# A fused low-rank update on one core: the first two stores wait for TensorE's third group instead of for their sums alone

## The chip, the core and the metric

The kernel runs on one core of a Trainium2 chip. Its time is the device time of one execution in microseconds (us); several executions are taken and their median counts. A profile of one further execution gives the trace. In it PE is TensorE (matmul), PEld its weight load, DVE is VectorE, ACT is ScalarE, POOL is GpSimd and SP is SyncE, which here computes nothing: it issues every transfer between the memory (HBM) and the on-chip buffer (SBUF). The transfers themselves are carried out by the core's 16 DMA engines.

## The reference

```python
batch, seq, d_model, r = 16, 512, 768, 16
# x: float32 [16, 512, 768], A: [768, 16], B: [16, 768], scale = 0.5

def reference(x, A, B, scale):
    lora = np.matmul(np.matmul(x, A), B)
    return (x + scale * lora).astype(np.float32)
```

The input x has 8192 rows of 768 float32 numbers, 25.2 MB. All of it is read once, and a result of the same size is written once. A and B are small.

## The kernel before

**Tiles and groups.** The 8192 rows are cut into 64 tiles of 128 rows, and eight tiles make a group, so there are eight groups (0 to 7). A tile takes 3 KB in each of the 128 partitions. SBUF holds 48 tiles of x at a time (`ROOM`); the last 16 tiles reuse the room of the first 16. Results are formed in place, in the room of their x.

**Transfers.** `LOADS` lists eight loads of 2, 6, 8, 8, 8, 16, 8 and 8 tiles (loads 0 to 7), `STORES` five stores of 8, 8, 16, 16 and 16 tiles (stores 0 to 4). A tile is 384 KB, so 8 tiles are 3072 KB and 16 tiles 6144 KB. Each transfer is one instruction of SP, issued in this order: loads 0 and 1, three pieces of A, B, loads 2 to 5, store 0, store 1, then load 6 (after store 0 has landed, s_out0), load 7 (after store 1 has landed, s_out1), then stores 2, 3 and 4. Loads 6 and 7 wait because they overwrite the tiles that stores 0 and 1 read. Store 0 holds group 0, store 1 group 1, store 2 groups 2 and 3, store 3 groups 4 and 5, store 4 groups 6 and 7. Load 5 brings groups 4 and 5, load 6 group 6, load 7 group 7.

**One group.** ACT and POOL narrow half a group each to float16 (L182, each waits for the group's load). DVE turns the eight tiles in blocks (L238). TensorE projects them with A in 24 matmuls (L269) and signals s_y. ACT spreads and scales the small result (L226, s_spread). TensorE then raises it with B, pair by pair: a group has four pairs of tiles (`PAIRS` is 4), four matmuls for each pair into one of two PSUM buffers (L290), and after each pair it raises the semaphore s_lora by one. DVE adds each pair to x in place (L243, `summed`). s_lora counts up over the whole kernel: 4 after group 0, 8 after group 1, 10 when pairs 0 and 1 of group 2 have been raised. TensorE takes the raising of group g in two halves, with half of the projection of group g + 1 behind each.

**Semaphores around the change.** `s_sum` is raised by DVE when the last pair of a store's groups has been added. `s_free[p]` tells TensorE that pair p has been added, so that its PSUM buffer may be overwritten. For the last pair of a group that ends a store, DVE raises s_sum instead, and SP passes it on: it waits for s_sum and then increments `s_free[PAIRS - 1]` (L145 and the lines around it). TensorE waits for that increment before it raises the second pair of the next group. So SP stands between DVE and TensorE at the end of groups 0, 1, 3 and 5, and both the wait and the increment are part of `store` in this kernel, ahead of the transfer's instruction (L146).

**SP's engine is in order.** What stands behind a wait on SP is not issued until the wait ends. The transfers it has issued run by themselves.

Of the kernel before, what the change touches and what calls it, by code (L numbers as in the profile page):

```python
# [28 lines left out]
def kernel(  # L29
# [20 lines left out]
    PAIRS = GROUP // 2  # L50
# [32 lines left out]
    def sem(name):  # L83
        sems.append(nc.alloc_semaphore(name))
        return sems[-1]
# [10 lines left out]
    def memory(t2, i, s, n):  # L96
        S = PARTS[i]
        return t2[ds(parts[i], S * P), :].rearrange("(p s) d -> p s d", s=S)[:, ds(s, n), :]

    def held(i, s, n):  # L100
        return tiles(where.index((i, s)), n)

    def tiles(t, n):
        return x_all[:, ds(t % ROOM, n), :]
# [15 lines left out]
    s_y, s_spread, s_lora = sem("s_y"), sem("s_spread"), sem("s_lora")  # L120
# [7 lines left out]
    STORES = [(0, 0, 8), (1, 0, 8), (2, 0, 16), (3, 0, 16), (4, 0, 16)]  # L128
# [6 lines left out]
    def on_sync(e):  # L135
        def load(k):
            ld = LOADS[k]
            e.dma_start(out=held(*ld), in_=memory(x2, *ld)).then_inc(s_load[k], 16)  # L138

        def store(k, done):  # L140
            st = STORES[k]
            e.wait_ge(s_sum, k + 1)
            if STORED[k] + 1 < NG:

                e.sem_inc(s_free[PAIRS - 1], 1)  # L145
            e.dma_start(out=memory(out2, *st), in_=held(*st)).then_inc(done, 16)  # L146

        load(0)
        load(1)
        e.wait_ge(s_ready, 1)  # L150
        blocks = A.rearrange("(c e) r -> c (e r)", e=64)
        for c in range(SETS):
            e.dma_start(
                out=a_rows[c : SET * SET : SET, :], in_=blocks[ds(c * SET, SET), :]
            ).then_inc(s_a, 16)
        e.wait_ge(s_brows, 1)
        e.dma_start(out=b_rows[0 : R * APART : APART, :], in_=B).then_inc(s_b, 16)
        for k in range(2, len(LOADS) - 2):
            load(k)

        for p in range(2, PAIRS):
            e.sem_inc(s_free[p], 1)
        store(0, s_out0)
        store(1, s_out1)
        e.wait_ge(s_out0, 16)
        load(len(LOADS) - 2)
        e.wait_ge(s_out1, 16)
        load(len(LOADS) - 1)
        for k in range(2, len(STORES)):
            store(k, s_out)  # L170

    here = set()
# [88 lines left out]
    def on_tensor(e):  # L261
# [57 lines left out]
        for p in range(PAIRS):  # L319
            raised(p)  # L320

    on_sync(nc.sync)
    on_gpsimd(nc.gpsimd)
    on_scalar(nc.scalar)
# [46 lines left out]
```

## Time and profile before

| what | value |
|---|---|
| time, median of 3 runs | 124.05 us (123.84 to 124.35) |
| the profiled execution's own time | 124.01 us |
| its span, first to last instruction | 122.2 us |
| busy: DVE | 81.7 us (67%) |
| busy: PE | 52.3 us (43%) |
| busy: ACT | 37.4 us (31%) |
| busy: POOL | 28.4 us (23%) |
| moved by the one DMA queue | 50.43 MB, 413 GB/s over the span |
| group 0's sums end on DVE | 32.7 us |
| group 1's sums end on DVE | 42.6 us |
| group 2's raising begins on PE | 43.2 us |
| last sums end on DVE | 101.2 us |

The span is the time between the first and the last recorded instruction; the 1.8 us beside it lie before and after. Busy shares are means over the whole span and say little by themselves: an engine can be busy 67% of the time and still set the pace for half of it. A transfer has three times that matter: its issue on SP, the moment its packets begin to move, and its landing, when its semaphore is complete. The list of DMA issues gives the first and the last; what lies between is read from the order in which transfers land and from the records of packets.

### The profile page before, as it was taken

The numbers are of one execution on the slowest core, as the hardware profiler recorded it, in microseconds if no ns is written. First come the engines' busy times: TensorE is split into PE (matmuls) and PEld (weight loads), VectorE is DVE, ScalarE is ACT, GpSimd is POOL, SyncE is SP. The second block draws the span as 40 slices with busy tenths as digits, with TensorE's granted clock in tenths as the row PEclk, the third lists the DMA queues.
The fourth block names the chain that finished last, engine by engine and source line by source line (L and its number), as shares of the span: only waits on it lengthen the run. The fifth ranks groups of instructions, "written<-read, shape, count | busy, mean of one in ns | idle before, by whom it ended". The sixth has DMA issues, their size and how long they took to land.

```text
span 122.2 us, 885 instructions
## 1 busy us (share of the span) xinstructions
PE 52.3 (43%) x322; PEld 30.4 (25%) x322; DVE 81.7 (67%) x42; ACT 37.4 (31%) x43; POOL 28.4 (23%) x24
## 2 busy tenths in 40 slices
PE   0000239487457547746745735974674340000000
PEld 0000026253233424424423322642442110000000
DVE  0002850599999999999999979999995991000000
ACT  4002938526408311835340093553004000000000
POOL 7631638026008001705300080440000000000000
PEclk9999999999999999999999996799999955555555
DMA  3999999999998996999999999999899899899890
GB/s 60 420 434 428 451 426 410 459 418 418 483 515 354 418 515 257 467 410 434 442 410 451 426 418 491 426 499 418 370 499 418 370 499 434 354 515 434 386 467 0
DMA packets 1928, 50.43 MB, mean 413 GB/s; under 512 B 236, under 2 KB 236, under 8 KB 392
## 3 DMA queue, kind: packets, MB, share of 16 engines
q1 hardware_dynamic: 1928, 50.43, 96.7%
HBM read 25.26 MB, written 25.17 MB: 413 GB/s over the span
## 4 chain that ended last, share of the span: by engine, by line
DMA 39%; DVE 28%; PE 7%; ACT 3%; issue 3%; POOL 2%; SPq 0%; DVEq 0%
DMA x_sb<-in_x_dram 20%; DMA out_dram<-x_sb 19%; DVE x_sb L243 18%; DVE xt L238 10%; PE ps_yt L269 5%; ACT xn L182 3%; POOL xn L182 2%; PE lora_ps L290 1%; SPq L138 0%; SPq L366 0%; DVEq L256 0%; SPq L145 0%; SPq L133 0%
## 5 line engine op out<-in xcount | busy, mean ns | idle before, releaser
L243 DVE TENSOR_TENSOR x_sb<-x_sb,lora_ps 128x1536 f32<-128x1536 f32 x32 | 53.7, 1733 | 1.4 <-PE lora_ps L290 1.4
L290 PE MATMUL lora_ps<-b_mm,y_bd 128*128 128x512 f16 (+1 forms) x128 | 26.5, 343 | 22.7 <-issue 15.0
L182 ACT CAST xn<-x_sb 128x3072 f16<-128x3072 f32 (+1 forms) x9 | 23.4, 2609 | 36.8 <-DMA x_sb<-in_x_dram 24.2
L238 DVE STREAM_TRANSPOSE xt<-xn 128x3072 f32<-128x3072 f32 (+1 forms) x9 | 27.0, 3004 | 6.7 <-PE ps_yt L269 5.5
L269 PE MATMUL ps_yt<-xt,w_bd 128*128 128x256 f16 x192 | 26.5, 291 | 11.5 <-DVE xt L238 11.5
L182 POOL CAST xn<-x_sb 128x3072 f16<-128x3072 f32 (+1 forms) x8 | 20.7, 2586 | 45.9 <-DMA x_sb<-in_x_dram 23.3
L269 PEld LDWEIGHTS ps_yt<-xt,w_bd 128*128 128x128 f16 x192 | 19.2, 102 | 19.5 <-issue 14.6
L290 PEld LDWEIGHTS lora_ps<-b_mm,y_bd 128*128 128x128 f16 x128 | 11.1, 100 | 36.0 <-issue 18.1
L226 ACT ACTIVATE y_bd<-ps_yt 32x256 f16<-32x256 f32 x32 | 12.0, 374 | 18.3 <-PE ps_yt L269 18.0
L231 DVE STREAM_TRANSPOSE a_t<-a_rows 32x1024 f32<-32x1024 f32 x1 | 1.9, 1945 | 11.4 <-DMA a_rows<-in_A_dram 11.4
L302 PE MATMUL lora_ps<-b_half,pick 128*128 128x512 f16 (+1 forms) x2 | 0.8, 504 | 12.6 <-POOL b_half L200 12.6
L302 PEld LDWEIGHTS lora_ps<-b_half,pick 128*128 128x128 f16 x2 | 0.1, 102 | 12.6 <-issue 12.6
L208 POOL COPY w_bd<-w_one 32x384 f16<-32x384 f16 x4 | 2.0, 500 | 0.2
L200 POOL CAST b_half<-b_rows 128x768 f16<-128x768 f32 x1 | 0.8, 827 | 4.4 <-DMA b_rows<-in_B_dram 4.4
L182 ACT ACT_TABLE_LOAD x1 | 1.3, 1283 | 0.9 <-SPq L133 0.9
L190 POOL MEMSET w_bd<- 128x1536 f32 x1 | 1.4, 1372 | 0.0
L202 POOL CAST w_one<-a_t 32x384 f16<-32x384 f32 x1 | 0.9, 852 | 0.9 <-DVE a_t L231 0.9
L187 POOL MEMSET a_rows<- 32x1024 f32 x1 | 0.9, 941 | 0.5 <-SPq L133 0.5
L219 ACT CAST b_mm<-lora_ps 128x768 f16<-128x768 f32 x1 | 0.8, 798 | 0.0
L188 POOL MEMSET b_rows<- 128x768 f32 x1 | 0.7, 727 | 0.0
L191 POOL MEMSET y_bd<- 128x512 f32 x1 | 0.5, 514 | 0.0
L193 POOL TENSOR_SCALAR_AFFINE_SELECT pick<-pick 128x128 f16<-128x128 f16 x1 | 0.3, 298 | 0.0
(5 smaller groups left out, 0.6 us busy)
## 6 DMA issues: line engine op xcount, KB each, us to landing
out_dram<-x_sb SPq DMA_DIRECT2D x3, 6144.0 KB, 23.6
x_sb<-in_x_dram SPq DMA_DIRECT2D x5, 3072.0 KB, 14.6
x_sb<-in_x_dram SPq DMA_DIRECT2D x1, 6144.0 KB, 42.2
out_dram<-x_sb SPq DMA_DIRECT2D x2, 3072.0 KB, 21.5
x_sb<-in_x_dram SPq DMA_DIRECT2D x1, 2304.0 KB, 9.9
x_sb<-in_x_dram SPq DMA_DIRECT2D x1, 768.0 KB, 4.7
a_rows<-in_A_dram SPq DMA_DIRECT2D x3, 16.0 KB
b_rows<-in_B_dram SPq DMA_DIRECT2D x1, 48.0 KB, 7.5
```

The costliest lines, as they stand in the source:

```text
L182: ins = copy(out=xn[:, ds(first, n), :], in_=tiles(t, n))
L187: e.memset(a_rows[0:Q], 0.0).then_inc(s_ready, 1)
L190: e.memset(w_bd.rearrange("p c k m -> p (c k m)").bitcast(fp32), 0.0)
L202: e.tensor_copy(out=w_one.rearrange("i (c e) k r -> i c e (k r)", c=SETS), in_=a_t[0:Q].rearrange("i k r (e c) -> i c e (k r)", c=SET)[:, ...
L208: e.tensor_copy(out=w_bd[ds(b * Q, Q), :, :, ds(b * Q, R)], in_=w_one).then_inc(s_w, 1)
L226: last = e.mul(out=y_bd[q, :, q], in_=y_ps[q, :, :], mul=sc)
L231: e.transpose(out=a_t[0:Q].rearrange("i k r c -> i (k r) c"), in_=a_rows[0:Q].rearrange("c (i k r) -> c (k r) i", k=2, r=R),).then_inc(s_r ...
L238: return e.transpose(out=ts[0], in_=ts[1])
L243: ins = e.tensor_tensor(out=xs, in0=xs, in1=lora[p % 2], op=mybir.AluOpType.add)
L269: mm = e.matmul(y_ps, w_bd[:, c, k, :], xv[:, :, c, :, k], start=(m == 0), stop=(m == MMS - 1),)
L290: mms.append(e.matmul(t[:, k, ds(n0, w)], y_bd[:, 2 * p + k, :], b_mm[:, ds(n0, w)], start=True, stop=True,))
L302: last = e.matmul(lora[0][:, 0, ds(n0, w)], pick.rearrange("p b r -> p (b r)"), b_half[:, ds(n0, w)], start=True, stop=True,)
```

## The change

The wait for a store's sums, and the increment that SP passes on to TensorE, become a function of their own, `summed`. For stores 0 and 1 both calls of `summed` now come first, then a wait until s_lora has reached 2 x 4 + 2 = 10, and only then are both stores issued. For stores 2 to 4 each `summed` stands directly ahead of its store, as it did. Transfers, sizes, buffers and the other engines' programs are the same.

```diff
+        def summed(k):
+            e.wait_ge(s_sum, k + 1)
+            if STORED[k] + 1 < NG:
+
+                e.sem_inc(s_free[PAIRS - 1], 1)
+
         def store(k, done):
             st = STORES[k]
-            e.wait_ge(s_sum, k + 1)
-            if STORED[k] + 1 < NG:
-
-                e.sem_inc(s_free[PAIRS - 1], 1)
             e.dma_start(out=memory(out2, *st), in_=held(*st)).then_inc(done, 16)
...
         for p in range(2, PAIRS):
             e.sem_inc(s_free[p], 1)
+        summed(0)
+        summed(1)
+
+
+        e.wait_ge(s_lora, 2 * PAIRS + 2)
         store(0, s_out0)
         store(1, s_out1)
         e.wait_ge(s_out0, 16)
...
         load(len(LOADS) - 1)
         for k in range(2, len(STORES)):
+            summed(k)
             store(k, s_out)
```

More of the change, by code (lines that the diff above doesn't have):

```diff
@@ L138, in load @@
             e.dma_start(out=held(*ld), in_=memory(x2, *ld)).then_inc(s_load[k], 16)
-        def store(k, done):
-            st = STORES[k]
+        def summed(k):
             e.wait_ge(s_sum, k + 1)
@@ L145, in store @@
                 e.sem_inc(s_free[PAIRS - 1], 1)
+        def store(k, done):
+            st = STORES[k]
             e.dma_start(out=memory(out2, *st), in_=held(*st)).then_inc(done, 16)
```

## The prediction

> **What bounds the kernel now.** I read the page first: the DMA row of its slices, the queue totals and the shares of the chain of waits.
>
> ```profile
> DMA  3999999999998996999999999999899899899890
> ...
> q1 hardware_dynamic: 1928, 50.43, 96.7%
> HBM read 25.26 MB, written 25.17 MB: 413 GB/s over the span
> ...
> DMA 39%; DVE 28%; PE 7%; ACT 3%; issue 3%; POOL 2%; SPq 0%; DVEq 0%
> ```
>
> The 16 DMA engines are busy 96.7% of the span, and one queue carries everything. The chain also has 28% of DVE, so it must be settled whether DMA or DVE sets the end. For that I looked at the timeline of SP's queue, which shows when each transfer is issued (a merged row gives its first start and its count; the second store of the x2 row starts at 42.74 by a closer window).
>
> ```profile
> 4.55 2.03 SPq L138 DMA_DIRECT2D x_sb<-in_x_dram  x4
> 32.82 10.25 SPq L146 DMA_DIRECT2D out_dram<-x_sb  x2
> 55.61 7.77 SPq L138 DMA_DIRECT2D x_sb<-in_x_dram  x2
> 63.50 38.04 SPq L146 DMA_DIRECT2D out_dram<-x_sb  x3
> ```
>
> Next the chain in order of time and the list of DMA issues (KB each, median us from issue to landing).
>
> ```profile
> 32.82 22.77 DMA out_dram<-x_sb
> 55.59 0.02 issue
> 55.61 14.59 DMA x_sb<-in_x_dram
> ```
>
> ```profile
> x_sb<-in_x_dram SPq DMA_DIRECT2D x1, 6144.0 KB, 42.2
> out_dram<-x_sb SPq DMA_DIRECT2D x2, 3072.0 KB, 21.5
> ...
> x_sb<-in_x_dram SPq DMA_DIRECT2D x1, 768.0 KB, 4.7
> ```
>
> Load 5 (the 6144 KB load, last of the four issued from 4.55) goes out near 6.1 and lands near 48.3. Store 0 lands at 32.82 + 22.77 = 55.59. Store 1 took 2 x 21.5 - 22.77 = 20.2 and landed at 42.74 + 20.2 = 63.0. Load 6 landed at 55.61 + 14.59 = 70.2. The steps are 7.3, 7.4 and 7.2 us, each for 3072 KB, which is 3.146 MB / 7.3 us = 431 GB/s. So **the queue serves transfers one behind the other, in the order of issue**: store 0 is issued at 32.82, yet its data moves only once load 5 is through. Sharing would have landed it earlier and load 5 later. The last place to look is the seam between load 5 and store 0: windows of 1 us (busy time of PE, PEld, DVE, ACT and POOL, clock, DMA share, GB/s; a packet counts wholly where it begins).
>
> ```profile
> 45.00:46.00 1.00, 0.00 (x0) 0.00 (x0) 1.00 (x2) 0.00 (x0) 0.00 (x0) 1.00 1.74 639
> 46.00:47.00 1.00, 0.93 (x9) 0.83 (x10) 1.00 (x1) 0.00 (x0) 0.00 (x0) 1.00 0.00 0
> 47.00:48.00 1.00, 0.95 (x9) 0.50 (x7) 1.00 (x2) 0.00 (x0) 0.00 (x0) 1.00 1.03 442
> ```
>
> The zero is no idle time. Load 5's packets are 49 KB; the packet records of the trace have its last 16, one for each DMA engine, beginning between 44.78 and 45.59 and ending between 47.03 and 47.98, and the first packet of store 0 begins at 47.03, in the instant at which the first engine is done. From there to 120.8 the engines are never without work: the last store is issued at 63.50 + 38.04 - 0.34 = 101.2, while store 3 still runs until about 105. DVE therefore has close to 4 us in hand at the end, and **the DMA queue sets the time**.
>
> **The change, part by part.** *The sums' signals* (two waits on s_sum, two increments of the fourth pair's s_free) stay where they were in SP's order, ahead of the new wait. TensorE gets them at 32.7 and 42.7 as before, so the third group's second pair isn't held up, and no wait closes a circle. Cost: nothing. *The new wait* (s_lora at 10) ends when the second pair of the third group has been raised. PE's timeline gives it:
>
> ```profile
> 43.19 1.46 PE L290 MATMUL lora_ps<-b_mm,y_bd 128*128 128x512 f16 x8 [1.67 <-issue]
> ```
>
> These eight matmuls are pairs 0 and 1 of that group; they end at 44.65, and the tenth s_lora event of the trace is at 44.67. So store 0 moves from 32.82 to about 44.72 (11.9 us later) and store 1 from 42.74 to 44.72 + 0.35 = 45.07 (2.3 us later). One wait instruction more costs SP some 0.05 us (the "issue" pieces of the chain), in a stretch where SP does nothing else. *Queued behind the wait* on SP are both stores, then load 6 behind store 0's landing and load 7 behind store 1's. Nothing else on SP is due before 55.6.
>
> *What hides the delay* is load 5: its last packets keep every DMA engine busy until 47.03 at the earliest, 47.03 - 44.72 = 2.31 us after the new issue. The one unknown is how long a store takes from its issue to its first packet when the queue behind it is about to run dry; the trace of before shows no store in that position. Nearest rows: load 0 was issued at 0.96 into an empty queue, and its first packet begins at 1.97, so **1.01 us** is the lower end. The upper end takes all of load 0's 4.7 us to landing except the movement itself (eight packets of 0.234 us for each engine, 1.87 us): 4.74 - 1.87 = **2.87 us**, though part of that lies behind the last byte. With the lower end store 0 is ready at 45.73, 1.3 us before any engine needs it: cost 0. With the upper end it is ready at 47.59, and engines that are done between 47.03 and 47.98 (mean near 47.4) idle 0.2 us on average, 0.56 us at worst. I take the lower end, because it is the same kind of event (issue to first packet), and keep +0.56 for the range.
>
> The Trainium skill speaks against the change: DMA: Bandwidth & Descriptors, section Rules for kernel authors, advises issuing a DMA early so that its fixed cost lies under other work, and its section Anatomy of one DMA puts that cost at about 2.0 us, fitted on another issuing path. By it, even if all 2.0 us came ahead of the first byte, store 0 would be ready at 46.72, an estimate from that page, and the sum would still be 0, with 0.3 us to spare. The load-0 row gives 2.87 us for the whole fixed part, more than the page, so the measured bound stays the upper end.
>
> *Below nothing.* Load 5's last packets take longer than its others. Most of its packets last 1.82 us; the last sixteen last 0.1 to 0.8 us more, about 0.44 on average (begin to end above). At the other seam from load to store, load 7 to store 2, the last packets are longer by about 0.1 us. If store 0, queued since 32.82, causes this by reading ahead, and if a store that comes at 45.7 does not, the seam gains up to 0.44 us. I can't exclude it and don't expect it: the store will again be queued before those packets end. I take 0.
>
> *Who is late next, if store 0 is.* A delay d at the seam shifts stores 0 and 1, load 6, load 7 and every later transfer by d, since the queue is full from there on. Load 6 is issued 7.4 us ahead of its turn, so no second gap opens. Group 6 waits for load 6 (POOL and ACT do now) and DVE ends d later, but the last store follows store 3, which is d later too. So d counts once, in full.
>
> Sum: 0 (signals) + 0 (wait) + 0 (stores, covered by load 5) = 0. The profiled execution took 124.01 us, of which 122.2 are the span and 1.8 lie around it; the median of the three runs is 124.05. I forecast **124.0 us**.
>
> **Rivals.** *The seam opens.* One mechanism, at 47.03: the store's start-up is longer than its 2.31 us of cover. It decides from there on, one us for each us beyond. For it: the issue now stands 2.3 us before need instead of 14, and load 0's start-up was measured with no other traffic. Against it: it must more than double the 1.01 us seen. Price: at 2.87 us some 0.2 to 0.56, 124.2 to 124.6. If a busy memory doubled load 0's whole fixed part to 5.7 us, the gap would be 3.4 us, 127.4. In the middle, at the whole 4.74 us, the gap is 2.4 and the time 126.4. Slower by over 0.5% (0.62 us) needs a start-up of about 2.9 us or more.
>
> *The queued store had been slowing the load.* Place: load 5's last packets. Price: -0.44 us, 123.6, or with the longest of the stretches gone -0.8, 123.2. For it: the stretch stands exactly at this seam. Against it: load 5's earlier packets, with the store queued behind them for 12 us, keep 1.82 us, and the stores' own 49 KB packets later take the same.
>
> *The change does nothing because the wait never holds.* The sums of group 1 are done at 42.65 and the new event comes at 44.67, so it holds store 1 for 2.0 us and store 0 for 12. That is excluded.
>
> **How the numbers follow.** Within 0.5% is about what a measurement of this kernel can tell from no change: 123.4 to 124.7. The forecast (nothing moves) has 0.65. The queued-store rival has 0.15; by its mean price it stays within 0.5%, and I give half of it to faster. The open seam has 0.20, of which 0.05 is the small gap of 0.2 to 0.56 us and 0.15 the larger one. Faster 0.07, same 0.78, slower 0.15. The range, 123.4 to 124.8, holds the forecast, the mean price of the second rival and the upper bound of the start-up; it leaves out the large gap and the longest stretches.
>
> **What would show it.** In the changed kernel SP's timeline should have two stores 0.35 us apart near 44.7 and load 6 still at 55.6. The first store should land near 55.6 after about 10.9 us, where it now takes 22.8. The share of the DMA engines in the windows around 47 should show no gap, and DVE's rows should stand where they do. Wrong would be: load 6 issued later than 56, which is the open seam, its size read off directly; or load 5 landing before 48.0 and load 6 issued before 55.2, which is the queued-store rival. A time outside 123.4 to 124.7 with store 0 landing at 55.6 would mean that something other than this seam moved.

## The result and the profile after

| | before | changed |
|---|---|---|
| median of 22 runs each | 124.06 us | 123.75 us |
| ratio of times | | 0.998, 95% interval 0.9971 to 0.999 |
| the profiled execution's own time, its span | 124.01, 122.2 us | 123.66, 121.8 us |

The changed kernel is 0.3 us faster. That is 0.2%, less than the 0.5% that was set as the bound of "no change", but over this many runs the interval lies clear of 1. The page, with the DMA row of its slices, the queue's total, the traffic and the shares of the chain of waits:

```profile
DMA  3999999999997996999999999997997998998990
...
q1 hardware_dynamic: 1928, 50.43, 96.9%
HBM read 25.26 MB, written 25.17 MB: 414 GB/s over the span
...
DVE 50%; PE 14%; issue 8%; DMA 8%; ACT 3%; SPq 0%
```

Bytes and packets are the same, and the queue is as full as it was. The chain now runs over DVE (50%) where it ran over DMA (39%). That sounds like a change of bound and isn't one: before, it passed through store 0's landing, which took 22.77 us from issue; this link is now 10.8 us long, and the chain follows DVE through the same stretch. The end is still the queue's: the last store is issued at 102.12, and store 3 keeps every engine busy until 104.99 at the earliest. The timeline of SP's queue:

```profile
4.57 2.02 SPq L138 DMA_DIRECT2D x_sb<-in_x_dram  x4
44.42 0.82 SPq L148 DMA_DIRECT2D out_dram<-x_sb  x2
55.26 7.75 SPq L138 DMA_DIRECT2D x_sb<-in_x_dram  x2
63.13 39.32 SPq L148 DMA_DIRECT2D out_dram<-x_sb  x3
```

Both stores go out at 44.42 and 44.82. Load 6 follows at 55.26, when store 0 has landed, 0.35 us earlier than before (55.61). The difference is therefore there by the seam between load 5 and store 0. The same 1 us windows as before (a packet counts wholly where it begins; the last two columns are DMA share and GB/s):

```profile
45.00:46.00 1.00, 0.20 (x2) 0.22 (x3) 1.00 (x2) 0.00 (x0) 0.00 (x0) 1.00 1.61 688
46.00:47.00 1.00, 1.00 (x11) 0.85 (x10) 1.00 (x1) 0.00 (x0) 0.00 (x0) 1.00 0.41 172
47.00:48.00 1.00, 0.95 (x7) 0.32 (x5) 1.00 (x2) 0.01 (x1) 0.00 (x0) 1.00 1.03 442
```

In the window from 46 to 47 nothing began before; now the first of store 0's packets do (172 GB/s). The packet records say why. Load 5's last sixteen packets begin at 45.22 in the mean in both kernels. They last 2.18 us before and 1.84 us after, where the other packets of that size last 1.82. They end at 47.40 and 47.06 in the mean: 0.34 us. Load 5 lands at 47.96 instead of 48.32.

Not all of it is kept. From here on a *turn* is a place in the queue where loads change to stores or back, and its *loss* is the time by which the packets in it last longer than others of their size, as a mean over the 16 engines. Before, load 5 to store 0 lost 0.38 us and load 7 to store 2 0.05 us. After, these lose 0.03 and 0.15 us, and store 1 to load 6 loses 0.05 us. The sum falls by 0.2 us only, and the mean landing of store 4 over the engines only from 120.45 to 120.32. But a transfer is done when its slowest engine is, and that one lands at 120.94 instead of 121.28. So most of the gain at the end, 0.34 us, is the slowest engine's. The time goes with that engine and not with the mean: in all the profiles of this document the execution takes 2.72 to 2.75 us longer than the slowest engine's landing of store 4. The losses below are means, so they locate a cost, but their sum doesn't give the time.

### The profile page after: what moved, and what is told of

The parts are those of the page before. It is cut to its first block, busy times and chain, and to the rows that moved or that the text cites. A ratio compares the mean times of both kernels' runs of the same rounds, so it can differ in the third digit from the quotient of the medians.

```text
span 121.8 us, 885 instructions
## 1 busy us (share of the span) xinstructions
PE 52.8 (43%) x322; PEld 31.0 (25%) x322; DVE 81.8 (67%) x42; ACT 37.5 (31%) x43; POOL 28.4 (23%) x24
## 4 chain that ended last, share of the span: by engine, by line
DVE 50%; PE 14%; issue 8%; DMA 8%; ACT 3%; SPq 0%
DVE x_sb L251 32%; DVE xt L246 18%; PE ps_yt L277 8%; DMA x_sb<-in_x_dram 8%; PE lora_ps L298 5%; ACT xn L190 3%; SPq L138 0%; SPq L374 0%; SPq L133 0%
## 5 line engine op out<-in xcount | busy, mean ns | idle before, releaser
L277 PE MATMUL ps_yt<-xt,w_bd 128*128 128x256 f16 x192 | 27.3, 297 | 11.6 <-DVE xt L246 11.6
```

What stands on the lines that cost most here:

```text
L277: mm = e.matmul(y_ps, w_bd[:, c, k, :], xv[:, :, c, :, k], start=(m == 0), stop=(m == MMS - 1),)
```

## The experiments

Theory Q, formed on seeing this: a store that is queued already when a load's last packets begin makes these last longer. The rivals are that something else about the early stores costs (their long time in the queue, or the second of them), that the size of the load's packets decides, and that the lengthening comes and goes by chance.

**Both stores at group 1's sums.**

```diff
         summed(0)
         summed(1)
-        e.wait_ge(s_lora, 2 * PAIRS + 2)
         store(0, s_out0)
```

> The new wait on s_lora is left out: both stores are issued when group 1's sums are done, near 42.7 us, 2 us before load 5's last packets begin (44.8 to 45.7). Theory Q (a store that is already queued when load 5's last packets begin makes them last longer): those packets take about 2.25 us again where the changed kernel has 1.82, the span goes back by 0.4 us, ratio to the kernel before 0.999 to 1.001. Rival T (it is the long time in the queue, from 32.8 us on, or store 0 being there while load 5 runs, that costs): packets near 1.82 us, ratio near 0.998. Rival N (the lengthening comes and goes from one execution to the next and the change has nothing to do with it): no pattern, time within 0.1% of the changed kernel's 123.75 us.

Measured: ratio 0.9993 (0.9982 to 1.0004). Its timeline of SP's queue and two of the windows:

```profile
42.39 0.82 SPq L148 DMA_DIRECT2D out_dram<-x_sb  x2
55.74 7.63 SPq L138 DMA_DIRECT2D x_sb<-in_x_dram  x2
```

```profile
45.00:46.00 1.00, 0.28 (x3) 0.27 (x4) 1.00 (x2) 0.00 (x0) 0.00 (x0) 1.00 1.79 639
46.00:47.00 1.00, 1.00 (x11) 0.81 (x9) 1.00 (x1) 0.00 (x0) 0.00 (x0) 1.00 0.00 0
```

The zero is back, load 6 is issued at 55.74, and load 5's last packets last 2.24 us. The stores were 2 us earlier than in the changed kernel and still 10 us later than before, so it isn't the long time in the queue that costs. (The interval holds 1 and overlaps the changed kernel's, so it is the packets rather than the time that decide here; the same goes for the next run.)

**Store 1 alone held back.**

```diff
         summed(0)
+        store(0, s_out0)
         summed(1)
         e.wait_ge(s_lora, 2 * PAIRS + 2)
-        store(0, s_out0)
         store(1, s_out1)
```

> Store 0 is issued at its sums again (32.8 us), store 1 alone waits for s_lora at 10. Theory Q: store 0 is queued when load 5's last packets begin, so they take about 2.25 us and the time is that of the kernel before, ratio 0.999 to 1.001. Rival S1 (store 1, the second store in the queue, is what lengthens them): packets at 1.82 us, ratio near 0.998. Rival N: no pattern.

Measured: ratio 0.9995 (0.9984 to 1.0005), last packets 2.27 us. Store 0 alone does it.

**A second profile of either kernel.** No edit.

> The kernel before once more, for a second profile. Theory Q: load 5's last sixteen packets again last about 2.25 us in the mean (0.1 to 0.8 us over the usual 1.82) and begin the same way near 45. Rival N: their lengthening differs by more than half from the first profile's 0.4 us.

> The changed kernel once more, for a second profile. Theory Q: load 5's last packets take 1.82 us again, mean lengthening under 0.1 us. Rival N: a lengthening of 0.2 us or more appears.

Measured: 124.03 and 123.73 us; last packets 2.16 us (spans 122.2) and 1.82 us (121.9). Two profiles of each kernel agree, which speaks against chance; the table of all profiles below bears it out. But the changed kernel's second profile lost 0.12 us at store 1 to load 6 and 0.31 us at load 7 to store 2, so what it gives back there varies.

**One pair earlier, and a little later.**

```diff
-        e.wait_ge(s_lora, 2 * PAIRS + 2)
+        e.wait_ge(s_lora, 2 * PAIRS + 1)
```

> Both stores wait for s_lora at 9 instead of 10, one pair earlier, near 43.8 us. With the start-up of 0.85 us seen when the seam was open, store 0 is ready near 44.65, just before the first of load 5's last packets begins (44.7 to 44.9) and 0.6 us before their mean. Theory Q (what is queued when a last packet begins counts): the lengthening is there again, 0.3 us or more, and the ratio 0.999 to 1.000. If only a store that is queued during the packet ahead of the last counts: no lengthening, ratio 0.997 to 0.998.

Measured: store 0 issued at 43.50, last packets 2.09 us, a lengthening of 0.27 us and so a little under the 0.3 expected, ratio 0.999 (0.9978 to 1.0001).

```diff
         e.wait_ge(s_lora, 2 * PAIRS + 2)
+        for _ in range(6):
+            e.sem_inc(s_pad, 1)
         store(0, s_out0)
```

`s_pad` is a spare semaphore for which nothing waits; the line that makes it is left out here and in the later edits.

> The changed kernel with six empty increments on SP behind the wait on s_lora, so both stores are issued 0.37 us later, near 44.9, and store 0 is ready near 45.7, when all of load 5's last packets have begun and 0.9 us before the first ends. If the window between too early and too late is wide: the changed kernel's time, ratio 0.997 to 0.998, no lengthening. If the run with the issue at 45.5, half of whose executions took 125 us or more, was slow because less than 1 us of cover is too little: some executions above 124.8 here too.

Measured: issued at 44.79, last packets 1.82 us, ratio 0.998 (0.9966 to 0.9994), no execution over 124.2. The lengthening in this profile has gone entirely, yet the median, 123.92 us, is no better than the changed kernel's. The later turns lost more in the profile (0.13 and 0.38 us), but that doesn't explain the median, for the profiled execution itself took only 123.51 us. Here the mean landing of store 4 is 120.44, as in the kernel before (120.45), and the slowest engine's is 120.79 instead of 121.28. It is the same in the second pair of profiles: 120.48 against 120.46 in the mean, 121.01 against 121.31 for the slowest. In these two the gain is wholly the slowest engine's, and how the turns' losses come to fall less on that engine isn't shown.

**Load 5 in two halves**, in the kernel before, so that its packets are of 24 KB.

```diff
-        ... (3, 0, 16), (4, 0, 8), (4, 8, 8)
+        ... (3, 0, 8), (3, 8, 8), (4, 0, 8), (4, 8, 8)
```

> The kernel before with load 5 cut into two loads of 8 tiles, so that its packets are of 24 KB (0.91 us) like load 7's; stores 0 and 1 are issued at their sums as before. Theory Q with packet size (what is lost is tied to the size of the load's last packet): the last packets of the second half are lengthened by 0.05 to 0.15 us, as load 7's are ahead of store 2, and the time falls by 0.3 us to about 123.75, ratio near 0.998. If the loss is fixed for a seam from load to queued store: 0.4 us of lengthening and ratio 0.999 to 1.001.

Measured: the turn lost 0.40 us, ratio 1.0005 (0.9996 to 1.0015). My guess on packet size falls: the loss is of the same size for packets half as large. But it isn't the last packet of each engine that is longer here (0.92 us, against 0.91 for the others). It is mostly the one ahead of it: these sixteen begin between 44.90 and 45.75, the stretch in which the 49 KB packets begin, and last 1.26 us in the mean. So the loss goes with the time ahead of the turn, some 2 us, and not with the place next to the store. Why load 7 to store 2 costs 0.05 us in the kernel before, with 24 KB load packets and a queued store too, this doesn't explain; the table below bears on it.

**Later still.** Three runs, to price the start-up and the open seam.

```diff
-        e.wait_ge(s_lora, 2 * PAIRS + 2)
+        e.wait_ge(s_taken, 4)
```

> Both stores wait for TensorE's fourth s_taken (second matmul of the next projection, 46.47 us in the trace of before) instead of s_lora at 10. This prices a store's start-up from issue to first packet, which the prediction bounded by 1.01 and 2.87 us. With 1.01 us the first packet of store 0 begins near 47.5, the engines (through between 46.7 and 47.5) stand idle for some 0.4 us in the mean, and the time is 0.4 us above the changed kernel's, near 124.1, ratio 1.000 to 1.002. With 2.87 us the first packet begins near 49.3 and the time is near 126.

Measured: median 124.93 us, ratio 1.0051 (1.0023 to 1.008). Five executions are at 123.86 to 124.16 and seven at 124.86 to 125.92; the ratio of 1.000 to 1.002 that was expected from a start-up of 1.01 us is missed. The profile, one of the lower group, has the issue at 45.49, no gap at the seam, last packets of 1.82 us, and then losses of 0.37 and 0.78 us at the two later turns.

```diff
-        e.wait_ge(s_lora, 2 * PAIRS + 2)
+        e.wait_ge(s_taken, 4)
+        for _ in range(8):
+            e.sem_inc(s_pad, 1)
```

> As the run that waited for the next projection's second matmul (issue at 45.5), with eight empty increments of a spare semaphore on SP behind the wait, 0.06 us each, so the issue stands at 46.0 and store 0 is ready near 46.85, when about a third of the engines have ended load 5. Theory A (an open seam puts the engines in step, and engines in step lose again at the later turns, as in the run where all of them had to wait: 0.8 and 1.0 us): a gap of only 0.1 to 0.2 us at 47 and 1 us or more at the turns near 60 and 75, time 125.0 to 126, ratio 1.008 or more. Rival: the gap alone counts, 124.0 to 124.2, ratio 1.000 to 1.001.

Measured: 125.59 us, ratio 1.0108 (1.0087 to 1.0128). The size that theory A gave is right and its reason isn't shown. The profile is of the slowest execution, 126.44 us: store 0 was issued at 45.98, its first packet begins at 46.83, the gap is 0.02 us in the mean, and store 0 lands on the 16 engines over 0.62 us, so they are not in step. And still the later turns lose 0.78 and 0.99 us. Windows of 60 to 64, before, changed, and this run:

```profile
60.00:64.00 4.00, 2.33 (x20) 1.54 (x18) 4.00 (x3) 1.50 (x4) 0.00 (x0) 1.00 0.99 424
```

```profile
60.00:64.00 4.00, 2.33 (x18) 1.40 (x16) 4.00 (x3) 1.50 (x4) 0.00 (x0) 1.00 0.97 412
```

```profile
60.00:64.00 4.00, 1.75 (x12) 0.72 (x9) 4.00 (x2) 1.50 (x4) 0.00 (x0) 1.00 0.97 332
```

The engines are as busy (0.97) and carry less: 332 GB/s. This is how a lengthened packet looks where no packet is missing; the share of busy time alone hides it. Load 6 lands late by it, and ACT's timeline shows it by the start of the narrowing that waits for load 6, changed kernel first:

```profile
69.91 2.75 ACT L190 CAST xn<-x_sb 128x3072 f16<-128x3072 f32 x1 [7.25 <-DMA x_sb<-in_x_dram]
```

```profile
71.33 2.75 ACT L193 CAST xn<-x_sb 128x3072 f16<-128x3072 f32 x1 [9.38 <-DMA x_sb<-in_x_dram]
```

```diff
-        e.wait_ge(s_lora, 2 * PAIRS + 2)
+        e.wait_ge(s_lora, 2 * PAIRS + 3)
```

> Both stores wait for s_lora at 11, the third pair of the third group (48.46 us in the trace of before), after load 5 is through. The seam opens: with a start-up of 1.01 us the first packet of store 0 begins near 49.5, 2.4 us after the mean end of load 5's packets (47.1), and the whole rest is later by that, near 126.1 us, ratio 1.017 to 1.022. With 2.87 us: 128, ratio 1.032. If something later absorbs the gap (DVE's 4 us in hand at the end would, if DVE and not the queue set the time): ratio under 1.005.

Measured: 127.17 us, ratio 1.0243 (1.0227 to 1.0259). Its SP row and windows:

```profile
47.44 0.82 SPq L148 DMA_DIRECT2D out_dram<-x_sb  x2
```

```profile
46.00:47.00 1.00, 0.94 (x8) 0.50 (x7) 1.00 (x2) 0.00 (x0) 0.00 (x0) 1.00 0.00 0
47.00:48.00 1.00, 0.41 (x3) 0.02 (x1) 1.00 (x1) 0.14 (x1) 0.11 (x1) 1.00 0.01 0
48.00:49.00 1.00, 0.75 (x5) 0.49 (x6) 1.00 (x2) 1.00 (x1) 1.00 (x1) 1.00 0.94 393
```

Here the window from 47 to 48 is idle from 47.39 on, where the last of load 5's packets ends; the zero of 46 to 47 belongs to packets that began earlier and run on. Store 0's first packet begins at 48.29, so a store's **start-up is 48.29 - 47.44 = 0.85 us**, as in the run before it (46.83 - 45.98). The gap is 1.3 us in the mean. Added to the kernel before's 124.1 it gives 125.4, less the 0.4 us of the loss that is gone 125.0; the median is 127.2. In size, what is missing is what the later turns lost, 0.82 and 1.00 us in the profile; that execution itself took 126.46 us, so the sum, 126.8, is of the right size and no more.

**Store 2 held back too.** First with a wait that leaves it queued before load 7's last packets, then with 30 empty increments more.

```diff
             summed(k)
+            if k == 2:
+                e.wait_ge(s_narrow, 12)
             store(k, s_out)
```

> The changed kernel, and store 2 too is held back, until s_narrow reaches 12 (group 6 narrowed, near 72.8 us), still 3 us before load 7's last packets end (76.4 to 77.2). Theory Q: store 2 is then still queued before those packets begin (near 75.5), so their lengthening of 0.05 to 0.15 us stays and the time is the changed kernel's, 123.75, ratio near 0.998; if the time in the queue counts instead, 0.1 us less. An open seam would need a start-up of 3.6 us and isn't expected.

Measured: ratio 0.9978 (0.9964 to 0.9992), 123.75 us, the changed kernel's time; load 7 to store 2 lost 0.13 us.

```diff
+                for _ in range(30):
+                    e.sem_inc(s_pad, 1)
```

> The changed kernel with store 2 held until s_narrow is 12 (72.6 us) and 30 empty increments more (1.8 us), so that it is issued near 74.4 and ready near 75.25, when load 7's last packets begin. Theory Q: the lengthening of load 7's last packets (0.14, 0.27 and 0.13 us in the profiles so far) goes, and the time falls by 0.1 to 0.2 us below the changed kernel's 123.75, ratio 0.996 to 0.997. Rival: the lengthening there has another cause, or the slowest engine doesn't gain by it: 123.75, ratio 0.998. If the issue comes too late in some executions, they are 1 us slower or more.

Measured: 123.62 us, five executions between 123.58 and 123.71, ratio 0.9961 (0.9948 to 0.9973). SP's timeline:

```profile
43.78 0.82 SPq L149 DMA_DIRECT2D out_dram<-x_sb  x2
55.37 7.92 SPq L139 DMA_DIRECT2D x_sb<-in_x_dram  x2
74.56 26.83 SPq L149 DMA_DIRECT2D out_dram<-x_sb  x3
```

Store 2 is issued at 74.56 and load 7's last packets are not lengthened. This version is clearly faster than the kernel before. That it beats the changed kernel isn't settled: the intervals 0.9948 to 0.9973 and 0.9971 to 0.999 overlap. Nor is its profile the proof of theory Q at this turn, for its stores 0 and 1 went out early (43.78; TensorE began group 2's raising at 42.28 in that execution, against 42.93) and lost 0.23 us at the first turn, and in profiles where that turn costs something the later one costs little anyway.

All profiles in the order of store 0's issue (us; "ready" is issue + 0.85, as measured in two of the runs; the losses are the three turns' as defined above, gaps left out):

| kernel | issue | ready | load 5's last packets | load 5 to store 0 | store 1 to load 6 | load 7 to store 2 |
|---|---|---|---|---|---|---|
| load 5 in two | 32.09 | 32.94 | (24 KB) | 0.40 | 0 | 0.05 |
| store 1 alone late | 32.40 | 33.25 | 2.27 | 0.46 | 0 | 0.13 |
| before, second | 32.68 | 33.53 | 2.16 | 0.36 | 0 | 0.06 |
| before | 32.82 | 33.67 | 2.18 | 0.38 | 0 | 0.05 |
| at group 1's sums | 42.39 | 43.24 | 2.24 | 0.55 | 0 | 0.03 |
| one pair earlier | 43.50 | 44.35 | 2.09 | 0.29 | 0 | 0.07 |
| store 2 at the last moment | 43.78 | 44.63 | 2.04 | 0.23 | 0 | 0 |
| changed | 44.42 | 45.27 | 1.84 | 0.03 | 0.05 | 0.15 |
| changed, second | 44.48 | 45.33 | 1.82 | 0 | 0.12 | 0.31 |
| store 2 late too | 44.64 | 45.49 | 1.82 | 0 | 0.07 | 0.13 |
| a little later | 44.79 | 45.64 | 1.82 | 0 | 0.13 | 0.38 |
| at the first matmuls | 45.49 | 46.34 | 1.82 | 0 | 0.37 | 0.78 |
| idle, then store | 45.98 | 46.83 | 1.82 | 0 | 0.78 | 0.99 |
| after the third pair | 47.44 | 48.29 | 1.82 | 0.06 | 0.82 | 1.00 |

(0 stands for 0.03 or less where nothing else is given.) Load 5's last packets begin between 44.5 and 45.8 in all of them but the run with load 5 in two. The fifth column falls from some 0.4 us to nothing as the store's readiness comes up to and passes through just that stretch. The single packets of the thirteen other runs say the same: of the 101 that began before store 0 was ready, 99 are not lengthened; the 13 that began up to 0.4 us after it are longer by 0.05 us in the mean, the 30 that began 0.4 to 1.2 us after it by 0.24, and the 64 that began later still by 0.39. This is theory Q, with a soft edge of about 1 us, and the profiles show it for this turn. For load 7 to store 2 they don't: in the early runs store 2, too, is queued long before, and that turn costs 0.03 to 0.13 us. The last two columns rise in nearly the same order, from nothing to 1.8 us together. So the change moves along a curve: too early costs 0.4 us once at the first turn, too late costs more, later. The low stretch in between holds the issues from 44.42 to 44.79; it begins after 43.78, where the first turn still lost 0.23 us, and ends before 45.49.

## Why the prediction held, and the step that failed

The time, 123.75 us, lies within 0.3 us of the 124.0 forecast and inside the range. But the forecast was that nothing moves, and something did: the number held because the term that was put at nothing is a small one. That the wait for s_lora at 10 falls into the narrow stretch between too early and too late is luck, as the prediction reckoned with no cost of being early and put the late edge elsewhere. Step by step:

- **The queue serves in order and sets the time**: held. Stores issued 11.6 us later moved their data at the same place in the queue, and every landing behind the seam moved with it.
- **Signals at no cost**: held. SP passes them on at 32.48 and 42.39, and DVE adds without a stop through groups 0 to 4.
- **Store 0 near 44.72, hidden under load 5**: held. It went out at 44.42, and the first engine needed it at 46.68: 2.26 us of cover against 2.31 forecast. The start-up is 0.85 us in the two runs that show it, below the 1.01 taken as the lower end; the 2.87 kept for the range is excluded. The Trainium skill gives some 600 ns to the first byte on this path (DMA: Bandwidth & Descriptors, Latency and other measured facts); the runs show 0.85 us from issue to first packet. The Trainium skill's advice to issue early (DMA: Bandwidth & Descriptors, Rules for kernel authors), weighed in the prediction, would have been right for the runs that issued at 45.49 and later and wrong by 0.3 us for this one.
- **"Below nothing ... I take 0"**: this step failed. The row was seen, the gain was bounded at 0.44 us, and it came: 0.34 us at the seam in the mean, 0.31 in the time. The reason for taking 0 was that the store "will again be queued before those packets end". What decides is whether it is queued before they *begin*: ready at 45.27, when nine of the sixteen had begun, it cost next to nothing (three of the other seven packets are longer, by 0.1 us). The mean lengthening was also put too high, at 0.44; over the sixteen records it is 2.18 - 1.82 = 0.36 us.
- **"So d counts once, in full"**: failed too, without effect on this result. The run with the gap of 1.3 us lost 1.8 us more at later turns, and a run with almost no gap lost as much. The rival with the open seam was priced too low for that reason, and its cost begins before the cover is used up: with 46.54 - 45.49 = 1.05 us of cover for 0.85 us of start-up no engine waited in the profile, and seven of the twelve executions were about 1 us slow.
- **Chances**: the rival of the queued store, given 0.15 against 0.65 for no move at all, is what happened. The argument held against it, that load 5's earlier packets keep 1.82 us, was true and beside the point, as only the packets of the last 2 us or so ahead of the turn are lengthened. Of the two signs set for it, load 5 landed before 48.0 (at 47.96), and load 6 was issued at 55.26, just past the 55.2 named; in the changed kernel's second profile, at 47.74 and 55.04, both are met.

What stays open is why a turn costs more later when the first one cost nothing. Something of how far an engine has run ahead seems to be carried from turn to turn, but no run here followed a single engine through the queue, and it is argued, not shown. Open too is why the first load-to-store turn costs 0.4 us with a queued store and the second hardly anything. That the changed kernel's slowest executions (124.36 and 124.40) are ones in which the stores fell outside the low stretch is likewise only argued; between the four profiles with this very wait the issue of store 0 lay at 43.78, 44.42, 44.48 and 44.64, so it could happen.

## What to carry to other kernels

Where one queue carries loads and stores and is full from end to end, the moment of issue of a queued transfer looks free, but the place where the direction turns is not: look there at how long single packets last, not at the busy share. A store that became ready about when the load's last packets began cost least here. Against the kernel before, the gain was 0.2%, the loss from being 1 us late 0.5%, and from 1.5 us late 1.1%, so such a wait should be tied to an event that moves with the transfer, and is worth it only where nothing larger is left.

## What the runs showed of the hardware

- At the turn from load 5 to store 0, a store that was queued in time lengthened the load's packets of the last 2 us by 0.23 to 0.55 us in the mean over the engines: the last packet with 49 KB (0.38), mostly the last but one with 24 KB (0.40). At the turn from load 7 to store 2 the same runs lost 0.03 to 0.13 us.
- From a store's issue on SP to its first packet 0.85 us pass, while fourteen of the sixteen engines were still on load 5 (45.98 to 46.83) and while none was (47.44 to 48.29).
- With a store that came when the engines were about to run dry or just had, the turns some 15 and 30 us later lost 0.4 to 0.8 and 0.8 to 1.0 us, where they otherwise lost 0 to 0.1 and 0 to 0.4, with the engines shown as busy all along (97% at 332 GB/s against 99% at 424).
- The execution ended 2.72 to 2.75 us after the slowest engine's landing of the last store in all fourteen profiles, while the mean landing could stand still (120.46 and 120.48) as the time fell by 0.3 us.
